# A decoder trunk in float32: the head casts older tiles before it modulates the newest, the bias rows are made at the start, and the fold's sums are copied one product later

## The chip, the cores and the metric

The kernel runs on one core of one Trainium2 chip. The metric is the device time of one execution in microseconds (us). Every time here comes from executions on the chip or from the profile of one of them.

## The reference

One layer of a decoder trunk on 2048 rows (tokens) of 1024 numbers, in float32, cut to what matters:

```python
mod = silu(c) @ w_ada + b_ada                 # one row of 3 * 1024
shift, scale, gate = split(mod, 3)
u = x * (1 + scale) + shift                   # (2048, 1024)
q, k, v, a_gate, p_in, p_gate, m_a, m_p = split(u @ w_in)
a = sliding_window_sink_attention(q, k, v, sinks, bias(rel_bias)) * silu(a_gate)
a = a @ w_attn_proj
p = grouped(multiscale_causal_pool(p_in), w_pool_mix)     # 4 groups of 256 x 256
p = (p * pool_scale * silu(p_gate)) @ w_pool_proj
y = ((sigmoid(m_a) * a + sigmoid(m_p) * p) @ w_out) * (1 + gate)
x = layer_norm(ALPHA * x + y)
```

The bias of attention depends on the distance of two tokens alone: 32 buckets of distances, one number for each bucket and head. `w_pool_mix` is small, and the kernel multiplies it into the pooling part of `w_in` once ("the fold"), so that no product is needed for it later.

## The kernel before

**Products.** A float32 operand is split into a high part (an ACT cast to the type fp32r) and a low part (a DVE subtraction). `mm3` adds three TensorE matmuls, hi x hi, hi x lo and lo x hi. The big products go through a scheme with seven products instead of eight for a 2 x 2 block matrix, so that sums of the blocks are needed on both sides. The moving sides are called B11, T1, T2, B21, T3, B22 and T4 ("sets"), each of four k tiles of 128 x 512, high and low. The still sides are the weights, two blocks of 128 columns at a time (a `Quad`), with three pairs of sums `first`, `second` and `third`, each split by one ACT cast and one DVE subtraction of 128 x 1024 into buffers named `w_set`; `mid` and `late` make the sums in between. A "product" below is one call of `product`: twelve matmuls of 128 x 512. The sequence is fixed (`front`, `back`, `ring`): a group is two quads, whose `front` makes four products (B11 and T1 for each), and whose `back` makes ten: T2 and B21 for each quad, T3 and B22 for each, then T4 for each.

**Order of the work.** After each product `tick()` runs the hooks that are written down for that place, among them all side work: the sums of the second half of x (`sums_to`, stored as k_hi and k_lo), the fold (`fold_parts`), the gate's modulation and the transposes of v (`turn`). `steps` places a list of (offset, function) from a start position, counted in ticks. The engines marked as ordered (`act`, `dve`, `pool`, `sp`, `pe`) keep the program's order; other instructions are placed by a scheduler when the program is built. Each engine then runs its own list in order and waits at semaphores. DMAs are issued from the queues of SP, POOL and ACT.

**The head** (`head`) makes the modulation and the sets for the first half of x. It goes through the eight k tiles. For tile k, TensorE makes the shift (sixteen small matmuls, `pe_modulation`) and DVE the scale (a reduction of 128 x 1024, in the trace CUSTOM_DVE_ANT_0, then a one-column addition). ACT then modulates the two halves of x (ACTIVATE, 128 x 512 twice). `closing(k - 2)` splits T of the tile two back, and `middle(k - 1)` makes the difference t of the halves of the tile before and splits its B. So in step k the order on ACT is: modulate k, cast T of k - 2, cast B of k - 1. Between them stand the first splits of the two opening quads (`pair_split`, after tile 1), their `mid`, the first four products and, at the end, `rest_sums`, the sums from which T3, T4 and B22 are split by hooks in the first group (ticks 1, 2 and 4). A copy of half of each of four tiles goes to memory by POOL's queue (b12_d, in the trace b_d).

**The bias rows** (`bias_rows`) are 32 small GpSimd operations on 16 partitions, one for each bucket, which fill a row of 384 numbers for each head (`et`), and a store of it to e_d; a hook at tick 3 of the first group runs them. Later hooks (`spread_bias`) spread e_d over the partitions.

**The fold** runs four times in the first phase (starts 14, 42, 70, 94). `fetch` loads the mix matrix (mr) and a half of the weights (wpt into a buffer named spare), `split` splits them, `fold` makes 48 short matmuls into the PSUM banks pv and pt, copies the sums out as st_hi (ACT) and st_lo (DVE) and stores these to wmix_d from POOL's queue. Buffers named c (five of them) serve st_hi, st_lo, mr, k_hi, k_lo, the gates and, in this version, the bias rows; two buffers named spare serve `sums_to`, the fold and the gate's modulation in turn.

Of the kernel before, what the change touches and what calls it, by code (L numbers as in the profile page):

```python
# [11 lines left out]
F32 = mybir.dt.float32  # L12
# [46 lines left out]
def kernel(  # L59
# [30 lines left out]
    def set_tile(pl, n):  # L90
        return pl.tile([P, 4, 2, CH], F32R, tag=f"set_{n}", name=f"set_{n}")

    sets = {n: set_tile(cp, n) for n in ("B11", "T1", "T2", "B21")}
    ident = cp.tile([P, P], F32, name="ident")
    mod = cp.tile([P, 24], F32, name="mod")
    nsink = cp.tile([P, HEADS], F32, name="nsink")
# [27 lines left out]
    def as32(ap):  # L124
        return ap.bitcast(F32)

    def low(engine, dst, src, hi):
        engine.tensor_tensor(dst, src, as32(hi), ALU.subtract)  # L128
# [85 lines left out]
    def sums_to(ph, store, i, load, work, b12):  # L214

        b = []

        def x(r, c):
            return b[r][:, c * CH : (c + 1) * CH]

        def fetch():
            b.extend((ph.spare(), ph.spare()))
            for r in range(2):
                load(b[r], r)

        def sub(out, a, c):
            return lambda: pool.tensor_tensor(x(*out), x(*a), x(*c), ALU.subtract)

        todo = [(0, fetch), (3, lambda: work(b[0], 0)), (3.5, lambda: work(b[1], 1))]
        todo += [(at, sub(*z)) for at, z in (  # L230
            (7.5, ((0, 1), (0, 1), (0, 0))),
            (9, ((1, 1), (1, 1), (0, 1))),
            (10.5, ((1, 0), (1, 0), (1, 1))),
            (12, ((0, 0), (1, 1), (0, 0))),
        )]
        for at, name, z in (
            (4, "B11", (0, 0)), (4.7, "B12", (0, 1)), (5.4, "B21", (1, 0)), (6.1, "B22", (1, 1)),
            (8.5, "T1", (0, 1)), (10, "T2", (1, 1)), (11.5, "T4", (1, 0)), (13, "T3", (0, 0)),
        ):
            if b12 or name != "B12":  # L240
                split, keep = kept_parts(ph, store[name][i], lambda z=z: x(*z))
                todo += [(at, split), (at + 1, keep)]
        return sorted(todo, key=lambda t: t[0])
# [377 lines left out]
                nc.scalar.copy(dst[:, 0, :], src)  # L621
                low(nc.vector, dst[:, 1, :], src, kk[kv * HD : kv * HD + HD, kv, 0, c0 : c0 + CH])

    def bias_rows(ph):
        rel = ph.t.tile([HEADS, BUCKETS], F32, tag="c", bufs=ph.bufs["c"], name="rel")
        nc.sync.dma_start(rel, relT)
        et = ph.t.tile([HEADS, ET], F32, tag="c", bufs=ph.bufs["c"], name="et")
        pool.memset(et, BIG)
        bk = buckets()
        for b in range(BUCKETS):  # L630
            ds = np.nonzero(bk == b)[0]
            if len(ds) == 0:
# [345 lines left out]
    def fold_parts(ph, g):  # L978

        m, r, w = [], [], []  # L980

        def fetch(half):
            if half == 0:
                r.append(ph.c("mr"))
                sp.dma_start(r[0], mix[g])
            r.append(ph.spare())
            sp.dma_start(r[-1], wpt[g, half])

        def split(half):
# [6 lines left out]
            act.copy(w[0], r[-1])  # L996
            low(dve, w[1], r[-1], w[0])

        def fold(half):
            mhi, mlo = m  # L1000
            hi, lo = w
            for i in range(0, 4, 2):
                acc = bank("pt" if i else "pv").rearrange("p (e c) -> p e c", e=2)
                for e in range(2):
                    for ct in range(2):
                        a0 = ct * CH + (i + e) * P
                        cols = slice(ct * 256, (ct + 1) * 256)
                        mm3(acc[:, e], hi[:, a0 : a0 + P], lo[:, a0 : a0 + P], mhi[:, cols], mlo[:, cols], ct == 0, ct == 1)
                src = acc.rearrange("p e (m d) -> p e m d", m=2)
                st = [ph.c(n, F32R).rearrange("p (m e d) -> p m e d", m=2, e=2) for n in ("st_hi", "st_lo")]  # L1010
                by = [x.rearrange("p m e d -> p e m d") for x in st]
                nc.scalar.copy(by[0], src)
                low(nc.vector, by[1], src, by[0])
                k = 4 * half + i
                for hl in range(2):
                    dst = wmix_d[2 * g : 2 * g + 2, :, hl, k : k + 2, :].rearrange("m p k d -> p m k d")
                    nc.gpsimd.dma_start(dst, as32(st[hl]))

        return (
            (0, lambda: fetch(0)),  # L1020
            (1, lambda: split(0)),
            (2, lambda: (fold(0), fetch(1))),
            (3, lambda: split(1)),
            (4, lambda: fold(1)),
        )

    def modulate(u, k):
# [28 lines left out]
    def head(ph):  # L1056
# [13 lines left out]
        act.dma_start(mod, bada)  # L1070
        act.dma_start(psc, pscale)
        act.dma_start(nsink, sinks.partition_broadcast(P))
        act.activation(sg, ct, AF.Sigmoid)
        dve.tensor_tensor(ct, ct, sg, ALU.mult)
        act.activation(late[0], cb, AF.Sigmoid)
# [24 lines left out]
        def modulation(k):  # L1100
            m = KT + k
            w = ws[k][1]
            dve.tensor_tensor_reduce(w, w, cb, 1.0, mod[:, m : m + 1], ALU.mult, ALU.add, mod[:, m : m + 1])
            dve.tensor_tensor(mod[:, k : k + 1], mod[:, k : k + 1], sums[k][:, 0:1], ALU.add)
            for x in xs[k]:
                act.activation(x, x, AF.Identity, bias=mod[:, k : k + 1], scale=mod[:, m : m + 1])

        def minus(dst, a, b):
            dve.tensor_tensor(dst, a, b, ALU.subtract)
# [35 lines left out]
        for k in range(KT):  # L1145
            load(k)
            if k < 2:
                grp[k].load(ph, False, sp, None)
        opening(0)
        opening(1)  # L1150
        middle(0)
        for q in grp:
            q.sum1(dve)
            starts.append(pair_split(ph, q.first(), act, dve))
        for k in range(2, KT):
            opening(k)
            closing(k - 2)
            middle(k - 1)
            if k in (2, 4):
                grp[k // 2 - 1].mid(pool, dve)  # L1160
            if 3 <= k < 7:
                products(k - 3)
            if k == 7:
                rest_sums(0)
        closing(6)
        middle(7)
        opened[0][3] = pair_split(ph, grp[0].second(), act, dve)
        closing(7)
        opened[1][3] = pair_split(ph, grp[1].second(), act, dve)
        for i in (3, 1, 2):  # L1170
            rest_sums(i)
        for q in grp:
            q.late(dve)
# [14 lines left out]
    def first_phase(ph, groups, turn, opened, cb, rest):  # L1188
        hooks = {}

        def at(group, pos, f):
            hooks.setdefault((group, pos), []).append(f)

        for g in range(4):
            steps(hooks, groups, (14, 42, 70, 94)[g], fold_parts(ph, g))
        for i in range(2):
            at(1, 1 + 2 * i, lambda i=i: turn(i))
        for j in range(KT):
            at(3 + j // 2, 3 + 5 * (j % 2), lambda j=j: spread_bias(j))
        for i in range(4):  # L1200
            ks = (i, 4 + i)
            todo = sums_to(
                ph,
                u1_d,
                i,
                lambda x, r, ks=ks: sp.dma_start(x, xt[1, ks[r]]),
                lambda x, r, ks=ks: modulate(x, ks[r]),
                True,
            )
            steps(hooks, groups, (1, 29, 57, 80)[i], todo)  # L1210
        for i in range(8):
# [160 lines left out]
```

## Time and profile before

| what | value |
|---|---|
| median of 3 runs | 1870.0 us (1867.99 to 1878.24) |
| the profiled execution | 1861.84 us |
| its span | 1860.1 us |
| PE (TensorE) busy | 1735.2 us, 93% |
| PEld (weight loads, beside PE) | 1436.4 us, 77% |
| DVE (VectorE) busy | 1315.5 us, 71% |
| ACT (ScalarE) busy | 938.5 us, 50% |
| POOL (GpSimd) busy | 935.5 us, 50% |
| DMA | 381.32 MB, mean 205 GB/s |

A line of the timeline reads: start and duration in us, engine, line of the program, operation, output <- input, shapes, count, and in brackets the engine's idle time before it and what ended it. The helper that records the ordered engines' operations is line 55, so most lines say L55, and the names of the tiles tell what it is. An entry such as "SPq" is the issue of a DMA on that queue. PE's busy time also covers time in which matmuls are queued but starved of weights.

### The profile page before, as it was taken

What the parts mean: (1) busy time and instruction counts of PE and PEld (TensorE: products, weight loads), DVE (VectorE), ACT (ScalarE), POOL (GpSimd) and SP (SyncE); (2) the same over time, 40 slices, a digit from 0 to 9 for tenths busy, and PEclk for the clock granted to TensorE, in tenths of its full rate; (3) what the DMA queues carried; (4) which work ended last, traced back from release to release, by engine and by line L of the source; (5) the groups of instructions that cost most, each with busy time, mean ns of one, the idle gap of its engine ahead of it and who ended that gap; (6) DMA issues with size and microseconds to landing.
All of it is one profiled execution on the core that took longest, in us unless ns stands there. A gap on an engine that the chain in (4) does not pass through costs nothing. (4 is left out here: it accounts for less than half of the span.)

```text
span 1860.1 us, 25320 instructions
## 1 busy us (share of the span) xinstructions
PE 1735.2 (93%) x8248; PEld 1436.4 (77%) x8248; DVE 1315.5 (71%) x2284; ACT 938.5 (50%) x1977; POOL 935.5 (50%) x758
## 2 busy tenths in 40 slices
PE   6689899989999999999999999999989989999996
PEld 6467777777888888787777788888867778777775
DVE  5776766544677787777666457777857887886886
ACT  3543434333777776544444457777724333422453
POOL 0454445433254677545445314556763785476543
PEclk9889999999999999999999999999999999999998
DMA  9245566766344447785777733544786574689432
GB/s 346 74 163 189 198 218 213 254 211 180 107 144 163 159 154 294 262 285 196 254 258 251 259 126 120 181 145 139 278 300 204 185 258 155 214 291 382 146 140 104
DMA packets 163571, 381.32 MB, mean 205 GB/s; under 512 B 19680, under 2 KB 23792, under 8 KB 163440
## 3 DMA queue, kind: packets, MB, share of 16 engines
q1 hardware_dynamic: 150560, 342.95, 52.9%
q0 software_dynamic: 10112, 33.06, 5.2%
q10 hardware_dynamic: 2768, 3.70, 0.9%
q8 instruction: 65, 1.06, 0.2%
q14 instruction: 66, 0.54, 0.1%
HBM read 244.35 MB, written 138.44 MB: 206 GB/s over the span
## 5 line engine op out<-in xcount | busy, mean ns | idle before, releaser
L55 PE MATMUL mm<-set_B,w_set 128*128 128x512 f32 x3240 | 804.1, 396 | 31.7 <-DVE w_set L128 24.3
L55 PEld LDWEIGHTS mm<-set_B,w_set 128*128 128x128 f32 x3240 | 602.2, 189 | 165.8 <-DVE w_set L128 33.5
L55 PE MATMUL lg<-set_T,w_set 128*128 128x512 f32 x2088 | 529.1, 403 | 61.9 <-ACT w_set L311 24.6
L55 PEld LDWEIGHTS lg<-set_T,w_set 128*128 128x128 f32 x2088 | 398.6, 193 | 168.9 <-ACT w_set L311 33.2
L128 DVE TENSOR_TENSOR w_set<-W,w_set 128x1024 fp32r<-128x1024 f32 x162 | 241.4, 1490 | 142.4 <-ACT w_set L311 137.2
L311 ACT CAST w_set<-W 128x1024 fp32r<-128x1024 f32 x162 | 169.3, 1049 | 239.0 <-PE mm L55 146.8
L55 PE MATMUL mm<-set_T,w_set 128*128 128x512 f32 x1080 | 269.0, 397 | 0.6 <-ACT set_T L55 0.3
L55 PEld LDWEIGHTS mm<-set_T,w_set 128*128 128x128 f32 x1080 | 202.3, 190 | 44.6 <-ACT set_T L55 1.5
L289 POOL TENSOR_TENSOR W<-W 128x512 f32<-128x512 f32 x56 | 81.3, 1451 | 158.5 <-DVE w_set L128 149.4
L283 POOL TENSOR_TENSOR W<-W 128x512 f32<-128x512 f32 x56 | 86.8, 1550 | 130.8 <-DVE w_set L128 114.4
L362 POOL TENSOR_TENSOR p<-p,u 128x512 f32<-128x512 f32 x58 | 98.8, 1705 | 104.5 <-DVE u L361 102.2
L55 DVE TENSOR_TENSOR o<-pv,o 64x128 f32<-64x128 f32 x256 | 72.4, 283 | 92.7 <-ACT o L55 89.9
L55 ACT ACTIVATE L<-L,nm 128x257 f32<-128x257 f32 (+1 forms) x256 | 127.2, 498 | 8.6 <-DVE nm L55 3.5
L55 DVE TENSOR_TENSOR k_lo<-spare,k_hi 128x512 fp32r<-128x512 f32 x88 | 90.0, 1029 | 47.0 <-ACT k_hi L55 14.8
L279 POOL TENSOR_TENSOR W<-W,A 128x512 f32<-128x512 f32 x56 | 83.8, 1496 | 74.9 <-DMA W<-in_win_dram 17.0
L55 DVE CUSTOM_DVE_ANT_0 L<-lg,bt,nsink 128x256 f32<-128x256 f32 (+1 forms) x256 | 111.6, 473 | 5.3 <-PE lg L55 1.3
L284 POOL TENSOR_TENSOR W<-W 128x512 f32<-128x512 f32 x56 | 90.0, 1607 | 13.4 <-DMA W<-in_win_dram 10.5
L55 POOL TENSOR_TENSOR w_set<-W,w_set 128x1024 fp32r<-128x1024 f32 x14 | 33.6, 2403 | 122.5 <-ACT w_set L55 89.6
L55 POOL TENSOR_TENSOR p<-nxt,pg 128x512 f32<-128x512 f32 x32 | 41.3, 1291 | 104.0 <-DVE sm L55 103.9
L55 ACT COPY o<-pv 64x256 f32<-64x256 f32 x128 | 47.2, 369 | 82.4 <-PE pv L55 80.3
L55 DVE TENSOR_TENSOR ptl<-pt,pth 128x512 fp32r<-128x512 f32 (+1 forms) x128 | 85.7, 670 | 1.7 <-ACT pth L55 1.6
L55 PE MATMUL lg<-kk,qs 128*128 128x256 f32 (+1 forms) x512 | 80.5, 279 | 0.0
(201 smaller groups left out, 2495.9 us busy)
## 6 DMA issues: line engine op xcount, KB each, us to landing
W<-in_win_dram SPq DMA_DIRECT2D x68, 256.0 KB, 3.7
w_set<-wmix_d SPq DMA_DIRECT2D x32, 512.0 KB, 5.3
A<-in_win_dram SPq DMA_DIRECT2D x34, 256.0 KB, 4.1
W<-in_win_dram POOLq DMA_DIRECT2D x34, 256.0 KB, 3.7
ag_d<-sig SPq DMA_DIRECT2D x32, 256.0 KB, 2.8
pg_d<-sig SPq DMA_DIRECT2D x32, 256.0 KB, 3.7
ma_d<-sig SPq DMA_DIRECT2D x32, 256.0 KB, 3.8
mp_d<-sig SPq DMA_DIRECT2D x32, 256.0 KB, 3.2
```

What stands on the lines that cost most here:

```text
L55: return lambda *args, **kw: self.tc.keep_in_program_order(op(*args, **kw))
L128: engine.tensor_tensor(dst, src, as32(hi), ALU.subtract)
L279: e.tensor_tensor(self.w[:, 1, :], self.w[:, 2, :], self.a22, ALU.add)
L283: e.tensor_tensor(x[:, 1, :], x[:, 1, :], x[:, 0, :], ALU.subtract)
L284: e.tensor_tensor(x[:, 2, :], x[:, 0, :], x[:, 2, :], ALU.subtract)
L289: e.tensor_tensor(x[:, 0, :], x[:, 0, :], x[:, 1, :], ALU.subtract)
L311: a.copy(by_two(hi), raw)
L362: nc.gpsimd.tensor_tensor(p5, p5, u2, ALU.add)
```

## The change

Three things are done.

1. In `head`, `modulation` no longer modulates x; a new function `modulate_x(k)` does, and it is called after `closing(k - 2)` and `middle(k - 1)`. The first splits of the two opening quads come after the casts of step 2 and no longer after tile 1; `mid` comes in steps 3 and 5, not 2 and 4. `rest_sums(0)` and `rest_sums(1)` come in steps 6 and 7, the other two after the loop. The hooks for T3, B22 and T4 move one tick forward, to ticks 0, 1 and 3.
2. `bias_rows` runs at the start of the head, right after the first small loads. It works in a tile that shares its place with the set T2, which is claimed only afterwards (`late_sets(cp, "T2")`), and loads its table through ACT's queue.
3. In `fold_parts`, `fetch(1)` comes one product after `fetch(0)`, ahead of the first split, and the copies and stores of the sums are a function `keep` of their own, called one product behind the matmuls. The starts become 13, 41, 69 and 92, so that the matmuls stand where they stood, but for the fourth fold, whose matmuls come one product earlier. In `sums_to`, the buffers are taken in the other order and row 1 is loaded first.

```diff
-    sets = {n: set_tile(cp, n) for n in ("B11", "T1", "T2", "B21")}
+    sets = {n: set_tile(cp, n) for n in ("B11", "T1", "B21")}
@@ sums_to
             b.extend((ph.spare(), ph.spare()))
-            for r in range(2):
+            b.reverse()
+            for r in (1, 0):
                 load(b[r], r)
@@
-    def bias_rows(ph):
-        rel = ph.t.tile([HEADS, BUCKETS], F32, tag="c", bufs=ph.bufs["c"], name="rel")
-        nc.sync.dma_start(rel, relT)
-        et = ph.t.tile([HEADS, ET], F32, tag="c", bufs=ph.bufs["c"], name="et")
+    def bias_rows():
+        room = cp.tile([P, 4 * D], F32, tag="set_T2", name="head_T2")
+        rel, et = room[0:HEADS, 0:BUCKETS], room[0:HEADS, D : D + ET]
+        act.dma_start(rel, relT)
         pool.memset(et, BIG)
@@ fold_parts
+        accs = []
         def fold(half):
...
+                accs.append((4 * half + i, acc))
...
+        def keep():
+            for k, acc in accs:
                 src = acc.rearrange("p e (m d) -> p e m d", m=2)
...
-                nc.scalar.copy(by[0], src)
-                low(nc.vector, by[1], src, by[0])
+                act.copy(by[0], src)
+                low(dve, by[1], src, by[0])
...
-                    nc.gpsimd.dma_start(dst, as32(st[hl]))
+                    pool.dma_start(dst, as32(st[hl]))
+            accs.clear()
-            (1, lambda: split(0)),
-            (2, lambda: (fold(0), fetch(1))),
-            (3, lambda: split(1)),
-            (4, lambda: fold(1)),
+            (1, lambda: fetch(1)),
+            (2, lambda: split(0)),
+            (3, lambda: fold(0)),
+            (4, lambda: (keep(), split(1))),
+            (5, lambda: fold(1)),
+            (6, keep),
@@ head
+        bias_rows()
+        late_sets(cp, "T2")
         act.activation(sg, ct, AF.Sigmoid)
...
+        def modulate_x(k):
             for x in xs[k]:
-                act.activation(x, x, AF.Identity, bias=mod[:, k : k + 1], scale=mod[:, m : m + 1])
+                act.activation(x, x, AF.Identity, bias=mod[:, k : k + 1], scale=mod[:, KT + k : KT + k + 1])
...
         opening(0)
+        modulate_x(0)
         opening(1)
         middle(0)
-        for q in grp:
-            q.sum1(dve)
-            starts.append(pair_split(ph, q.first(), act, dve))
+        modulate_x(1)
         for k in range(2, KT):
             opening(k)
             closing(k - 2)
             middle(k - 1)
-            if k in (2, 4):
+            if k == 2:
+                for q in grp:
+                    q.sum1(dve)
+                    starts.append(pair_split(ph, q.first(), act, dve))
+            modulate_x(k)
+            if k in (3, 5):
                 grp[k // 2 - 1].mid(pool, dve)
             if 3 <= k < 7:
                 products(k - 3)
-            if k == 7:
-                rest_sums(0)
+            if k > 5:
+                rest_sums(k - 6)
...
-        for i in (3, 1, 2):
+        for i in (3, 2):
             rest_sums(i)
@@ first_phase
-            steps(hooks, groups, (14, 42, 70, 94)[g], fold_parts(ph, g))
+            steps(hooks, groups, (13, 41, 69, 92)[g], fold_parts(ph, g))
...
-        for n, f in zip((1, 2, 4), rest):
+        for n, f in zip((0, 1, 3), rest):
             at(0, n, f)
-        at(0, 3, lambda: bias_rows(ph))
```

More of the change, by code (lines that the diff above doesn't have):

```diff
@@ L995, in split @@
             w[:] = ph.split(), ph.split()
-            act.copy(w[0], r[-1])
-            low(dve, w[1], r[-1], w[0])
+            act.copy(w[0], r[1 + half])
+            low(dve, w[1], r[1 + half], w[0])
+        accs = []
         def fold(half):
@@ L1011, in fold @@
                 by = [x.rearrange("p m e d -> p e m d") for x in st]
-                nc.scalar.copy(by[0], src)
-                low(nc.vector, by[1], src, by[0])
-                k = 4 * half + i
+                act.copy(by[0], src)
+                low(dve, by[1], src, by[0])
                 for hl in range(2):
                     dst = wmix_d[2 * g : 2 * g + 2, :, hl, k : k + 2, :].rearrange("m p k d -> p m k d")
-                    nc.gpsimd.dma_start(dst, as32(st[hl]))
+                    pool.dma_start(dst, as32(st[hl]))
+            accs.clear()
         return (
             (0, lambda: fetch(0)),
-            (1, lambda: split(0)),
-            (2, lambda: (fold(0), fetch(1))),
-            (3, lambda: split(1)),
-            (4, lambda: fold(1)),
+            (1, lambda: fetch(1)),
[4 more added lines that the diff above has]
+            (6, keep),
         )
```

## The prediction

> **What bounds the kernel now.** I read the page first, then the busy time by stretches, then the timeline of the first 140 us engine by engine, then what ended TensorE's idle time in the first phase.
>
> ```profile
> span 1860.1 us, 25320 instructions
> 40.00:50.00 10.00, 9.48 (x55) 7.91 (x54) 6.17 (x11) 4.78 (x8) 0.55 (x1) 0.94 0.50 196
> 50.00:60.00 10.00, 2.74 (x21) 2.49 (x19) 5.82 (x13) 5.09 (x8) 0.00 (x0) 0.74 0.00 0
> 60.00:70.00 10.00, 6.40 (x17) 4.64 (x18) 10.00 (x16) 6.33 (x11) 0.00 (x0) 0.58 0.00 1
> 80.00:90.00 10.00, 5.00 (x18) 3.56 (x18) 8.94 (x13) 1.82 (x3) 10.00 (x29) 0.95 0.26 89
> ```
>
> The columns are stretch, length, busy PE, PEld, DVE, ACT, POOL, granted clock, DMA share, GB/s. Most of the span belongs to TensorE, but here it is idle: 7.3 us of 50 to 60, 3.6 of 60 to 70, 5.0 of 80 to 90. The DMA share from 50 on is 0, so loads do not bound the first hole. Neither DVE nor ACT is full there; they wait for each other. In 80 to 90 POOL is full, for the only time in the table. All edits lie in this stage or at the four folds, so the sum is made there; everything behind it stands in the same order.
>
> One step k of the head, and where the steps end:
>
> ```profile
> 50.02 1.28 DVE L55 CUSTOM_DVE_ANT_0 head_kk<-head_kk,cb,mod 128x1024 f32<-128x1024 f32 x1
> 51.41 1.52 ACT L55 ACTIVATE head_vv<-head_vv,mod 128x512 f32<-128x512 f32 x2 [2.71 <-DVE mod L55]
> 52.84 0.60 ACT L55 CAST set_T<-t 128x512 fp32r<-128x512 f32 x1
> 53.47 0.69 DVE L55 TENSOR_TENSOR set_T<-t,set_T 128x512 fp32r<-128x512 f32 x1 [2.09 <-ACT set_T L55]
> 54.08 0.68 DVE L55 TENSOR_TENSOR t<-A,t 128x512 f32<-128x512 f32 x1
> 54.68 0.69 DVE L55 TENSOR_TENSOR set_B<-head_kk,set_B 128x512 fp32r<-128x512 f32 x1
> 55.28 1.28 DVE L55 CUSTOM_DVE_ANT_0 head_kk<-head_kk,cb,mod 128x1024 f32<-128x1024 f32 x1
> 61.75 0.69 DVE L55 TENSOR_TENSOR set_T<-t,set_T 128x512 fp32r<-128x512 f32 x1
> 64.83 4.23 PE L55 MATMUL lg<-set_T,w_set 128*128 128x512 f32 x10 [1.41 <-DVE w_set L55]
> ```
>
> A step is 55.28 - 50.02 = 5.26 us. DVE reduces (1.39 to the start of the modulation), stands 2.09 us while ACT first modulates tile k and only then casts the older T tile, and subtracts three half tiles, 0.60 us apart (53.47 to 55.28 is 1.81). The ten matmuls at 64.83 are the first work TensorE gets behind the head, and DVE's subtraction of w_set releases them.
>
> **The head's order of casts.** In the changed program ACT casts T of k-2 and B of k-1 before it modulates k. Both inputs are there since the step before, so the casts run under DVE's reduction, the modulation runs under DVE's three subtractions, and the 2.09 goes. What is late next is DVE itself: 1.39 + 1.81 = 3.20 us a step. ACT's own step, 1.52 + 0.60 + 0.60, is 2.7, so it keeps up. Two quad splits also move behind step 2, and the `mid` subtractions to steps 3 and 5. For these:
>
> ```profile
> 20.65 3.58 PE L55 MATMUL lg<-ct,head_T 128*128 128x1 f32 x16 [2.86 <-DMA head_T<-in_wadat_dram]
> 20.69 0.68 DVE L55 TENSOR_TENSOR W<-W,A 128x512 f32<-128x512 f32 x1
> 26.56 1.28 DVE L55 CUSTOM_DVE_ANT_0 head_T<-head_T,cb,mod 128x1024 f32<-128x1024 f32 x1
> 31.82 1.28 DVE L55 TENSOR_TENSOR W<-W 128x512 f32<-128x512 f32 x2
> 33.03 1.28 DVE L55 CUSTOM_DVE_ANT_0 head_T<-head_T,cb,mod 128x1024 f32<-128x1024 f32 x1
> 34.48 0.33 SPq L55 DMA_DIRECT2D head_vv<-in_xt_dram  x1
> head_vv<-in_xt_dram SPq DMA_DIRECT2D x2, 512.0 KB, 10.7
> ```
>
> The two splits hold DVE from 20.69 to 26.56, 5.87 us, now while it waits for tile 2's weights. Moved, they lose that cover. Step 2 cannot finish before TensorE's sums for it do, 20.65 + 3.58 = 24.2, 24.4 with the addition; three subtractions make 26.2, the splits 32.1. So step 3 starts at 32.1 against 33.03, only 0.9 sooner. From there: five steps at 3.20 are 16.0; two `mid` pairs at 1.21 (31.82 to 33.03) are 2.4; `rest_sums` 0 and 1, four half tiles, are 2.4. DVE reaches the last-but-one T subtraction at 32.1 + 20.8 = 52.9. The same count for before, 33.03 + 5 x 5.26 + 1.21 + 1.20, gives 61.7, the row's 61.75. Gain so far 8.8 us. Loads: tile 7's x lands at 34.48 + 10.7 = 45.2, and its step begins at about 48.5, so they stay hidden, by 3 us. TensorE then starts at 64.83 - 8.8 = 56.0.
>
> **The bias rows and the rest of the splits.**
>
> ```profile
> 72.76 3.41 POOL L362 TENSOR_TENSOR p<-p,u 128x512 f32<-128x512 f32 x1 [27.07 <-DVE u L361]
> 76.13 1.21 DVE L128 TENSOR_TENSOR w_set<-W,w_set 128x1024 fp32r<-128x1024 f32 x1
> 77.05 2.92 PE L55 MATMUL lg<-set_T,w_set 128*128 128x512 f32 x12
> 78.95 11.27 POOL L55 TENSOR_SCALAR et<-rel 16x1 f32<-16x1 f32 x32
> 82.27 1.30 DVE L55 TENSOR_TENSOR set_B<-A,set_B 128x512 fp32r<-128x512 f32 x2
> 83.02 2.82 PE L55 MATMUL mm<-set_B,w_set 128*128 128x512 f32 x11 [2.82 <-DVE set_B L55]
> 88.49 4.15 PE L55 MATMUL lg<-set_T,w_set 128*128 128x512 f32 x10 [2.18 <-DVE w_set L128]
> 90.25 0.62 ACT L55 CAST k_hi<-spare 128x512 fp32r<-128x512 f32 x1 [2.29 <-POOL et L55]
> 100.75 0.63 PE L55 MATMUL mm<-set_B,w_set 128*128 128x512 f32 x2
> 209.89 1.30 POOL L55 TENSOR_TENSOR spare<-spare 128x512 f32<-128x512 f32 x1
> ```
>
> The bias rows, 32 operations in 11.27 us on POOL, go to the start of the head. The issue of two b12 stores and the `mid` loads stand behind them there; those loads are issued at about 36 and later, so POOL has room. The rows are made in the place that the set T2 takes later, whose first write comes after 40 us; their store is long done by then. Their small table load goes to ACT's queue ahead of the first sigmoid, in the shadow of the first weights.
>
> At the first group of products the splits of T3 and B22 move one product earlier. B22's wait of 2.82 goes, but the built order now has all of T3, B22 and T4 ahead of the third pair's w_set on DVE, and a gate product that needs the second quad's B21. From 56.0 DVE does 25 half tiles at 0.60 (15.0) and two w_sets at 1.2: the pair is ready at 73.4. TensorE's four products, 77.05 - 64.83 = 12.2, end at 68.2. A new wait of 5.2 us takes the place of 2.82 and 2.18. After it ten matmuls cost 4.15, as after 88.49, and five products follow at 2.70 (92.64 to 100.75 is three): 73.4 + 17.7 = 91.1 against 100.75. Gain 9.7.
>
> A rule that speaks against the move: the Trainium skill, SBUF — State Buffer, section "Who interferes with whom", says that a VectorE instruction with two SBUF inputs and a GpSimd instruction that reads SBUF block each other for a whole instruction. The trace has it for large tiles, POOL taking 3.41 at 72.76 where the same shape takes 1.30 at 209.89. For the small rows it does not: DVE's two-input pair at 82.27 took 1.30 in the midst of them, 0.65 each. If the rule held DVE for a row of 0.35 (11.27 / 32) at each of some eight operations in the head's first 20 us, the sum would be up to 2.8 us worse; by the row it is 0, which I take.
>
> **Folds and the first group behind.**
>
> ```profile
> 115.16 3.75 PE L55 MATMUL lg<-set_T,w_set 128*128 128x512 f32 x10 [1.82 <-DVE w_set L128]
> 127.34 1.22 PE L55 MATMUL lg<-set_T,w_set 128*128 128x512 f32 x2 [4.82 <-ACT w_set L311]
> 136.95 0.69 DVE L128 TENSOR_TENSOR st_lo<-pt,st_hi 128x512 fp32r<-128x512 f32 x1 [0.75 <-ACT st_hi L1012]
> 138.88 0.60 PE L55 MATMUL pt<-ident,vt 128*128 128x128 f32 x4
> 212.79 0.39 SPq L55 DMA_DIRECT2D spare<-in_wpt_dram  x1
> 221.14 0.73 PE L55 MATMUL lg<-set_T,w_set 128*128 128x512 f32 x2 [2.92 <-ACT w_set L311]
> 312.99 0.73 PE L55 MATMUL lg<-set_T,w_set 128*128 128x512 f32 x2 [1.58 <-ACT w_set L311]
> 394.30 0.73 PE L55 MATMUL lg<-set_T,w_set 128*128 128x512 f32 x2 [3.42 <-ACT w_set L311]
> ```
>
> At each fold TensorE waits for a w_set cast that stands on ACT behind the fold's own split. The first such wait is 4.82, where the others are 2.92, 1.58 and 3.42: the chain of k_hi that the bias rows held up (2.29 at 90.25) ends late there. Without them I take the 2.92 for it, a gain of 1.9 (ends 0 and 4.82), and half of the 1.82 at 115.16, 0.9. The fold's loads move one store pair earlier in SP's queue. The spare that they need is free at 209.89 + 1.30 = 211.2, where the load goes out at 212.79: up to 1.6 sooner, at three folds up to 4.8 in all, at least 0. I take half, 2.4. The copies of the sums: in the built order the same neighbours stand before and after them on ACT, so they cost and bring nothing.
>
> **The sum.** 9.7 + 2.8 + 2.4 = 14.9 us. The profiled execution took 1861.84 (span 1860.1), which becomes 1847; it is 8 under the median of 1870.0, so against that I forecast 1855.
>
> **The rivals.** First, the gain is spent in DVE's queue. The pair that I put at 73.4 sits behind operations that POOL can stretch, as its own 3.41 shows for the other side. If T3 starts no sooner than now, at 77.05, the group still loses its two later waits: 77.05 + 17.7 = 94.7, a gain of 6, and with the chains behind as late as now the time is 1864. For it: DVE was full from 60 to 70. Against it: POOL has two operations there. 0.17; the case that the new order leaves no trace at all is counted here.
>
> Second, slower: the copies held back. If they do run a product later, the next writer of the two PSUM banks waits. Now the last copy ends at 136.95 + 0.69 = 137.64 and the transposes into that bank run at 138.88, a room of 1.2 us. A product is 2.70; if each of eight folds costs a whole one, 21.6 eat the 12.5 of the other parts: 1879. It decides from 1.6 us a fold. Against it: the unchanged neighbours on ACT. 0.08.
>
> **How the numbers follow.** My forecast has 0.75. Its top gain is 9.7 + 1.8 + 4.8 + 4.8, 21 us, or 1849. The three runs lie between 1868 and 1878, so a median of as many can lie some 4 to 6 us off: the range is 1843 to 1868, from that top gain less 6 to the first rival plus 4. Only the second rival is left out. The bound of what a measurement can tell is 0.5%, 9.4 us: faster 0.74, same 0.18, slower 0.08.
>
> **What would show it.** Right: no 2.09 wait for set_T from step 3 on, steps of 3.2 us, TensorE's ten matmuls near 56, one wait of about 5 us near 68 to 74 for w_set, none near 83, front products at about 91. Wrong: steps still over 4 us, the pair later than 77, or waits in front of the transposes at the folds.

## The result, and the profile after

The changed kernel takes 1850.26 us (median of 4 runs, 1849.77 to 1854.1), before in the same comparison 1868.99 (median of 4, 1861.73 to 1878.24): a ratio of 0.9917, 95% interval 0.9895 to 0.9939, or 0.8% faster. The forecast was 1855, with a gain of 14.9 us; the medians differ by 18.7, and the ratio, by which all runs are compared here, makes 15.5 of 1869 (11.4 to 19.6 by its interval). The profiled execution took 1849.77 us.

First the busy time by stretches of the kernel after (the columns are those of the prediction's fence):

```profile
span 1848.0 us, 25300 instructions
...
50.00:60.00 10.00, 6.09 (x14) 4.31 (x15) 10.00 (x16) 8.06 (x14) 0.00 (x0) 0.51 0.00 1
60.00:70.00 10.00, 8.75 (x38) 6.89 (x36) 8.74 (x16) 6.63 (x12) 5.00 (x2) 0.98 0.45 159
80.00:90.00 10.00, 10.00 (x45) 8.18 (x44) 9.60 (x10) 5.11 (x10) 4.85 (x4) 1.00 0.32 117
```

From 50 to 60 DVE is now full, where it was busy 5.82 of 10, and TensorE is busy 6.09 and no longer 2.74. From 80 to 90 TensorE has no hole at all, and POOL is half free.

The timeline of the kernel after, from the head to the end of the first group's ten products. (They are made by `back`; the prediction calls them front products. The row at 91.86 is the first product behind them.)

```profile
9.04 7.97 POOL L55 TENSOR_SCALAR head_T<-head_T 16x1 f32<-16x1 f32 x32 [7.37 <-DMA head_T<-in_relT_dram]
...
42.99 1.29 DVE L55 CUSTOM_DVE_ANT_0 head_kk<-head_kk,cb,mod 128x1024 f32<-128x1024 f32 x1
...
44.48 0.69 DVE L55 TENSOR_TENSOR set_T<-t,set_T 128x512 fp32r<-128x512 f32 x1
...
47.50 1.28 DVE L55 CUSTOM_DVE_ANT_0 head_kk<-head_kk,cb,mod 128x1024 f32<-128x1024 f32 x1
...
55.13 4.63 PE L55 MATMUL lg<-set_T,w_set 128*128 128x512 f32 x10 [1.20 <-DVE w_set L55]
...
74.20 4.06 PE L55 MATMUL lg<-set_T,w_set 128*128 128x512 f32 x10 [5.45 <-DVE w_set L128]
...
91.86 2.94 PE L55 MATMUL mm<-set_B,w_set 128*128 128x512 f32 x12
```

The subtraction for set_T at 44.48 has no wait in brackets; before, it stood 2.09 us there. This step has two half tiles of `rest_sums` in it, so 47.50 - 42.99 = 4.51 is 3.31 without them (0.60 each). TensorE starts its ten matmuls at 55.13 (forecast 56.0, before 64.83). One wait of 5.45 follows (forecast 5.2), and the ten products end at 91.86 (forecast 91.1, before 100.75). This part came out as it was reckoned.

Then the waits at the folds in the kernel after:

```profile
117.70 1.22 PE L55 MATMUL lg<-set_T,w_set 128*128 128x512 f32 x2 [5.08 <-ACT w_set L312]
...
151.72 0.73 PE L55 MATMUL mm<-set_B,w_set 128*128 128x512 f32 x2 [1.70 <-ACT w_set L312]
153.24 4.63 PE L55 MATMUL mm<-set_B,w_set 128*128 128x512 f32 x10 [0.80 <-DVE w_set L128]
...
215.27 0.73 PE L55 MATMUL lg<-set_T,w_set 128*128 128x512 f32 x2 [3.09 <-ACT w_set L312]
...
251.16 4.14 PE L55 MATMUL mm<-set_B,w_set 128*128 128x512 f32 x10 [0.85 <-DVE w_set L128]
...
398.02 0.39 PE L55 MATMUL pv<-mhi,w_set 128*128 128x256 f32 x1 [0.54 <-ACT w_set L55]
```

The 4.82 in front of the first fold did not become 2.92; it is 5.08. Behind the second half of the first fold stands a wait that was not forecast, 1.70 and 0.80, and the ten matmuls behind it take 4.63 us. In the kernel before, the row at that place shows one wait of 1.15, and 2.57 us for the ten matmuls:

```profile
162.13 2.57 PE L55 MATMUL mm<-set_B,w_set 128*128 128x512 f32 x10 [1.15 <-DVE w_set L128]
```

The same pair of waits stands behind the second and third fold. The 3.42 in front of the fourth fold is gone. So the total came out near the forecast, but its terms behind 92 us did not, and the experiments ask about those.

### The profile page after: what moved, and what is told of

The parts are those of the page before. It is cut to its first block, busy times and chain, and to the rows that moved or that the text cites. A ratio compares the mean times of both kernels' runs of the same rounds, so it can differ in the third digit from the quotient of the medians.

```text
span 1848.0 us, 25300 instructions
## 1 busy us (share of the span) xinstructions
PE 1732.7 (94%) x8248; PEld 1437.6 (78%) x8248; DVE 1312.4 (71%) x2284; ACT 942.6 (51%) x1977; POOL 928.6 (50%) x758
## 5 line engine op out<-in xcount | busy, mean ns | idle before, releaser
L55 PE MATMUL lg<-set_T,w_set 128*128 128x512 f32 x2088 | 523.0, 400 | 49.5 <-ACT w_set L312 18.2
L285 POOL TENSOR_TENSOR W<-W 128x512 f32<-128x512 f32 x56 | 90.0, 1610 | 12.1 <-DMA W<-in_win_dram 9.5
L55 ACT CAST k_hi<-spare 128x512 fp32r<-128x512 f32 x88 | 53.6, 616 | 55.2 <-POOL spare L55 20.3
```

The lines of the kernel that those rows point to most:

```text
L55: return lambda *args, **kw: self.tc.keep_in_program_order(op(*args, **kw))
L285: e.tensor_tensor(x[:, 2, :], x[:, 0, :], x[:, 2, :], ALU.subtract)
```

## The experiments

Each kernel ran beside the kernel before, in the same comparison. Its ratio is to that.

| run | what is in it | median us | before | ratio, 95% interval |
|---|---|---|---|---|
| e1 | new head, early bias rows | 1851.95 | 1867.53 | 0.9921 (0.9899 to 0.9944) |
| e2 | fold part alone | 1869.44 | 1867.53 | 1.0004 (0.9985 to 1.0022) |
| e3 | bias rows alone | 1869.04 | 1867.53 | 1.0014 (0.9996 to 1.0032) |
| e4 | new head alone | 1854.15 | 1867.53 | 0.9932 (0.9906 to 0.9958) |
| e5 | the whole change again | 1854.31 | 1869.43 | 0.9912 (0.9892 to 0.9932) |
| e6 | change, copies with their fold | 1849.14 | 1869.43 | 0.9897 (0.9878 to 0.9917) |
| e7 | change, stores from ACT's queue | 1854.34 | 1869.43 | 0.9917 (0.9901 to 0.9932) |
| e8 | e1, folds split a product later | 1839.90 | 1869.43 | 0.9841 (0.9824 to 0.9858) |
| e9 | change, stores placed freely | 1844.55 | 1865.55 | 0.9892 (0.9876 to 0.9909) |
| e10 | change, T3, B22, T4 a tick later | 1851.67 | 1865.55 | 0.9927 (0.9912 to 0.9942) |
| e11 | e8, fourth fold a product sooner | 1834.65 | 1865.55 | 0.9823 (0.9799 to 0.9848) |
| e12 | e11 with the ticks of e10 | 1833.90 | 1865.55 | 0.9827 (0.9807 to 0.9847) |

**The three parts, one at a time (e1 to e4).** The theory that these began with: the head brings the gain, and the fold's late copies hold the buffers named c and give some of it back.

```diff
# e1: of the change, without
-            b.reverse()
-            for r in (1, 0):
+            for r in range(2):
... fold_parts as before
-            steps(hooks, groups, (13, 41, 69, 92)[g], fold_parts(ph, g))
+            steps(hooks, groups, (14, 42, 70, 94)[g], fold_parts(ph, g))
# e2: before, with these same parts as changed
# e3: before, with bias_rows() at the start of the head and its place in T2
# e4: e1, with bias_rows(ph) at tick 3 of the first group as before
```

> The changed kernel with the fold, the order of sums_to and the fold's starts as before; only the new head and the early bias rows are left of the change. In the changed kernel the lead over before is 10.5 us at the first fold's short matmuls and 6.0 at the second fold's. Theory A (the copies held back keep the buffers named c, so the lead is lost behind each fold): here the lead stays between 9 and 11 at the second and third fold, the wait in front of the mm product behind the second half of each fold is 1.0 to 1.3 us and not 1.70 + 0.80, and the fourth fold's wait of 3.4 is back; the time is 1847 to 1853, within 4 us of the changed kernel on either side. Theory B (the lead itself is what is lost, because the loads behind it are no earlier): the lead falls to about 6 at the second fold here too, and the time is 1853 to 1858.

> The kernel before with only the fold's part of the change (copies one product later, both loads early, starts 13, 41, 69 and 92, sums_to in the other order). Theory A: 1 to 2 us are lost behind each of the first three folds and about 5 come back at the fourth: within 3 us of before in all, with new waits behind the second half of the first three folds. Theory B: nothing is lost behind the folds and the gain at the fourth stands alone: 4 to 6 us faster than before. The prediction's reckoning was 2.4 faster.

> The kernel before with only the bias rows made at the start of the head. By the prediction the chain of k_hi starts 2.3 us earlier, the 1.82 before the product at 115 halves and the 4.82 at the first fold becomes 2.92: 2.8 us faster. Rival: the chain at the first fold is held by the buffers named c and not by POOL, so that the 4.82 stays as in the changed kernel (5.08): 0 to 1 us faster. If the 32 small operations hold up the head's first steps, the first products come later than 64.83: slower by up to 2.8.

> The kernel before with only the new order in the head (older tiles cast first, splits after step 2, mid in steps 3 and 5, T3, B22 and T4 split a product earlier); the bias rows stay on GpSimd at tick 3 of the first group. By the prediction the ten T2 matmuls start near 56 and the first group's front of products ends about 9 us sooner: 8 to 10 us faster than before. Rival (the bias rows, now in the midst of the moved sums, hold them up): the pair for the third sums comes 2 us or more later than 74 and the time is 5 to 7 us under before.

The head alone makes 0.9932, 12.7 us of 1867.53 (interval 7.8 to 17.6); the 8 to 10 expected lie inside, below the middle. The head with the bias rows makes 0.9921, the whole change 0.9912 and 0.9917: the fold part adds nothing that can be told, and alone it makes 1.0004. The 4 to 6 us of e2's theory B are excluded by its interval (its lower end is 2.8 us). The bias rows alone bring nothing (1.0014; its lower end allows 0.7 us). What became of their 2.8 is seen in the timeline of e3, ACT's chain and then TensorE at the first fold:

```profile
119.11 0.62 ACT L55 CAST k_hi<-spare 128x512 fp32r<-128x512 f32 x1 [2.16 <-DMA u_T_split<-k_hi]
121.16 0.62 ACT L55 CAST mhi<-mr 128x512 fp32r<-128x512 f32 x1 [1.43 <-DMA mr<-in_mix_dram]
...
123.95 1.04 ACT L311 CAST w_set<-W 128x1024 fp32r<-128x1024 f32 x1
...
125.04 1.22 PE L55 MATMUL lg<-set_T,w_set 128*128 128x512 f32 x2 [5.65 <-ACT w_set L311]
```

k_hi waits for a store to give a buffer back, the fold's split waits for the load of the mix matrix, and the cast of w_set that TensorE needs stands behind both. GpSimd is not in this chain. The wait is 5.65, not 2.92.

In e1 the wait behind the second half of the first fold is back to one of 1.45:

```profile
149.73 2.57 PE L55 MATMUL mm<-set_B,w_set 128*128 128x512 f32 x10 [1.45 <-DVE w_set L128]
```

So the new waits belong to the fold part. e2 has them too, 1.54 + 0.79, 2.17 + 0.86 and 2.79 + 0.53 behind the first three folds, and 0.84 where 3.42 stood in front of the fourth. Loss and gain come to nothing in sum, which fits theory A of e2 in the waits and the time; what makes the waits is asked next.

In the change the wait in front of the first fold has a longer chain than in e3. The last cast of k_hi ahead of the fold's split, on ACT:

```profile
114.61 0.62 ACT L55 CAST k_hi<-spare 128x512 fp32r<-128x512 f32 x1 [6.74 <-DMA u_T_split<-k_hi]
```

The store that it waits for was issued at 108.94, behind the first two loads of the fold. When this cast is done, the mix matrix and the weights are there, and no further wait stands before the cast of w_set at 116.60. In e4 the waits of the same chain are 1.63 for the store, then 1.76 and 1.38 for the two loads. Nothing here separates the bias rows from the rest in time: e1 and e4 differ by 2.2 us, with intervals that overlap.

**What in the fold part costs (e5 to e7, e9).** e5 repeats the change so that it stands in the same comparison.

```diff
# e6: the change, with
-            (3, lambda: fold(0)),
-            (4, lambda: (keep(), split(1))),
-            (5, lambda: fold(1)),
-            (6, keep),
+            (3, lambda: (fold(0), keep())),
+            (4, lambda: split(1)),
+            (5, lambda: (fold(1), keep())),
# e7: the change, with
-                    pool.dma_start(dst, as32(st[hl]))
+                    act.dma_start(dst, as32(st[hl]))
```

> The changed kernel once more, on the same chip and beside the same runs of before as the three that follow, to have it in one comparison with them. 0.990 to 0.994 of before; the lead over before's profile at the second fold's short matmuls (226.31 there) is about 6, and ten matmuls behind the wait of 1.70 + 0.80 take 4 us and more, not 2.6.

> The changed kernel with one thing undone: each copy and store of the fold's sums is made right behind its own fold, not one product later; the early second load and the starts stay. Theory A (the held copies put their stores behind GpSimd's next sum, which waits for a load, so the buffers named c come free too late): the waits of 1.70 + 0.80, 1.83 + 0.85 and 2.78 + 0.53 behind the second half of the first three folds go back to one of 1.0 to 1.3, the product after them to 2.6 us, and the lead over before at the second fold stays at 10 us or more; first attention matmul 3 to 6 us sooner than in the changed kernel. Theory B (the early load or the other starts do it): the waits stay, and the time is the changed kernel's within 1 us.

> The changed kernel with the stores of the fold's sums issued from ACT's queue and no longer from GpSimd's; the copies stay one product late. Theory A: the stores of the second half go out some 2 us behind their copies and not behind GpSimd's sum, 3 to 4 us sooner than now; the activation that waited 9.15 us for a buffer waits less than 6, and the waits 1.70 + 0.80 shrink to below 1.5 in sum. Rival (a copy one product late is itself too late, on whatever queue its store goes): the waits stay within 0.5 us of what they are. What the issues cost on ACT is small: four of 0.7 us for each half.

e5 has the new waits again (1.46 + 0.80 and 4.09 us for the ten matmuls). Its lead at the second fold is 226.31 - 217.21 = 9.1 and not 6. The expectation took a place in one profile for a property of the kernel: two executions of the same program stand 3 us apart there. From here on waits are compared, and stretches that begin and end at the same work.

e6 went against theory A at the first fold. With the copies called right behind their fold, waits of 1.49 + 0.80 still stand there; behind the second there are one of 1.52 and one of 1.21. The time, 0.9897, is 3 us below that of e5, with intervals that overlap. The timeline of GpSimd in e6 at the first fold shows why:

```profile
139.63 1.65 POOL L280 TENSOR_TENSOR W<-W,A 128x512 f32<-128x512 f32 x1 [10.97 <-DVE st_lo L55]
141.22 0.72 POOL L55 DMA_DIRECT2D wmix_d<-st_hi  x1
```

(The end of this wait is put down to a subtraction on DVE; at e6's second fold, where it is 10.82, to the load of A, as in the change.) Neither the copies nor the stores are sooner than in the change. The two copies of the first fold's second half start 1.64 and 3.95 us behind the half's first matmul in e6, 1.63 and 3.98 in the change, and 1.64 and 3.96 in the kernel before: called a product later, they came no later at the first three folds, as the prediction had it. The first store goes out 7.6 us behind the half's start in e6, 6.9 in the change, and 2.5 before. It stands behind GpSimd's sum for the next weights, because `pool` keeps the written order where before the scheduler placed the stores (`nc.gpsimd`). In e7, where the stores leave by ACT's queue, the wait behind the second half is gone (no wait from 132 to 197 us), and the activation that waited 9.15 us for a buffer waits 0.91. But now ACT's casts stand behind the issues, and TensorE waits between the halves instead:

```profile
129.46 0.74 PE L55 MATMUL lg<-set_T,w_set 128*128 128x512 f32 x2 [2.11 <-ACT w_set L312]
131.12 4.08 PE L55 MATMUL lg<-set_T,w_set 128*128 128x512 f32 x10 [0.92 <-DVE w_set L128]
```

Its time is that of the change. A third theory, C, came out of these two: neither the copies nor the loads make the waits behind the folds, but the place of the stores in GpSimd's queue. e9 tests it with one word.

```diff
# e9: the change, with
-                    pool.dma_start(dst, as32(st[hl]))
+                    nc.gpsimd.dma_start(dst, as32(st[hl]))
```

> The changed kernel with one word changed: the stores of the fold's sums are left to the scheduler again, as before, and no longer bound to the written order of GpSimd. The copies still come one product late. In the built order three of the four stores of a second half then stand ahead of GpSimd's sum for the next weights, not behind it. Theory C (it is the place of the stores in GpSimd's queue that costs, not the late copies): the activation that waited 9 us for a buffer named c waits less than 4, the waits 1.70 + 0.80, 1.83 + 0.85 and 2.78 + 0.53 shrink to one of 1.0 to 1.5 each, the product after them takes 2.6 us, and the first attention matmul comes 3 to 6 us before the changed kernel's 458.9 to 460.3. Rival (the copies are too late themselves): the waits stay, and the time is that of the changed kernel within 1 us.

The view of waits from 120 to 460 us (engine and tile that waits, what it waits for, us in total, times, longest), first of the change, then of e9:

```profile
POOL W L280 <- DMA A<-in_win_dram: 35.4, 4, 10.7
...
ACT sig L517 <- DMA wmix_d<-st_lo: 27.8, 3, 9.8
...
DVE c L387 <- DMA wmix_d<-st_hi: 17.1, 3, 6.3
...
POOL wmix_d L55 <- ACT st_hi L55: 4.2, 4, 3.3
```

```profile
POOL wmix_d L1023 <- ACT st_hi L55: 28.5, 10, 7.5
...
ACT sig L517 <- DMA wmix_d<-st_lo: 4.7, 3, 2.0
...
POOL W L280 <- DMA A<-in_win_dram: 4.5, 4, 1.4
...
DVE c L387 <- DMA wmix_d<-st_hi: 1.4, 2, 0.8
```

The chain is in these lines. GpSimd waits up to 10.7 us for a load; the stores stand behind it; ACT and DVE wait for the buffers that the stores read; the cast of w_set that TensorE needs stands behind them on ACT. With the stores ahead of the sum, the waits of ACT and DVE for these buffers fall from 44.9 us in sum to 6.1. GpSimd's own wait does not shrink, it changes place: 28.5 us ahead of the stores and 4.5 ahead of the sum, 33.0 in all, where the change has 4.2 and 35.4. The timelines at the first fold, of the change and then of e9:

```profile
138.82 1.29 POOL L280 TENSOR_TENSOR W<-W,A 128x512 f32<-128x512 f32 x1 [10.59 <-DMA A<-in_win_dram]
140.06 0.73 POOL L55 DMA_DIRECT2D wmix_d<-st_hi  x1
...
149.12 0.63 ACT L517 ACTIVATE sig<-c 128x512 f32<-128x512 f32 x1 [9.15 <-DMA wmix_d<-st_lo]
```

```profile
134.99 0.73 POOL L1023 DMA_DIRECT2D wmix_d<-st_hi  x1 [7.45 <-ACT st_hi L55]
...
139.42 1.29 POOL L280 TENSOR_TENSOR W<-W,A 128x512 f32<-128x512 f32 x1 [1.37 <-DMA A<-in_win_dram]
...
140.12 0.63 ACT L517 ACTIVATE sig<-c 128x512 f32<-128x512 f32 x1 [0.87 <-DMA wmix_d<-st_lo]
...
151.32 2.57 PE L55 MATMUL mm<-set_B,w_set 128*128 128x512 f32 x10 [1.57 <-DVE w_set L128]
```

The first store goes out 2.5 us behind the start of the fold's second half (132.47) and no longer 6.9 (133.18 to 140.06). TensorE's wait is one of 1.57 and the ten matmuls take 2.57; behind the second and third fold it is one of 0.77 and one of 1.23. The copies start 1.63 and 3.98 us behind the half's first matmul, as in the change. So theory C holds for the mechanism. In time e9 makes 0.9892 against 0.9912 and 0.9917, some 4 us with intervals that overlap: the direction is as expected, the size is not settled. In the profile its first attention matmul comes at 445.81, 13 us before e5's 458.9 and more than expected; it also ran the stretch from 300 to 400 at a granted clock of 1.00 where e5 had 0.98.

**The wait in front of the folds (e8, e11).** The chain of e3 says that w_set waits on ACT for the fold's own load. e8 leaves the loads where they are and takes the splits a product later, on the base of e1.

```diff
# e8: e1, with
-            (1, lambda: split(0)),
-            (2, lambda: (fold(0), fetch(1))),
-            (3, lambda: split(1)),
-            (4, lambda: fold(1)),
+            (2, lambda: (split(0), fetch(1))),
+            (3, lambda: fold(0)),
+            (4, lambda: split(1)),
+            (5, lambda: fold(1)),
...
-            at(1, 1 + 2 * i, lambda i=i: turn(i))
+            at(1, 2 + 2 * i, lambda i=i: turn(i))
# e11: e8, with the fourth fold's start at 93 and not at 94
```

> The new head and the early bias rows with the fold of before, but each fold's loads are issued where they were and its splits and short matmuls come one product later (and the two transposes of v one product later too). It asks what the wait in front of each fold is: w_set stands on ACT behind the fold's own split, which waits for a load that is issued 5 to 6 us before. If that is so, the waits of 3.52, 2.83, 1.51 and 3.50 us in front of the four folds fall below 1 each, the products behind them go from about 4 us to 2.6, and the first attention matmul comes 8 us or more before 454.8; 1842 to 1848 us. Rival (the next product's cast is late in any case): the waits move by one product and stay as long; 1850 to 1854.

> As the run with the splits a product later, but the fourth fold starts at 93 and not at 94, so that its short matmuls are where they were before and only its loads and the stores come sooner. There a wait of 3.08 stood behind that fold, and the twelve matmuls after it took 5.99. If the fold's stores, a product later than before, held the buffers named c there, the wait falls to 0.5 to 1 and the product to 3 us, and the first attention matmul comes at 434 to 437 instead of 440.75: 0.981 to 0.983 of before. Rival (the wait goes back to the front of the fold, 3.5 us as in the kernel before): no gain, 0.984 to 0.986.

The timeline of TensorE at the product in front of the first fold, e1 and then e8:

```profile
114.01 0.79 PE L55 MATMUL lg<-set_T,w_set 128*128 128x512 f32 x2 [3.52 <-ACT w_set L311]
```

```profile
109.46 0.61 PE L55 MATMUL lg<-set_T,w_set 128*128 128x512 f32 x2
110.36 2.57 PE L55 MATMUL lg<-set_T,w_set 128*128 128x512 f32 x10 [0.29 <-DVE w_set L128]
```

In e8 the waits of 3.52, 2.83 and 1.51 in front of the first three folds are gone, and 3.50 in front of the fourth is 0.74. The first attention matmul comes at 440.75, 14.0 us before e1's 454.79, and the time is 1839.9 us, a little under the 1842 to 1848 expected; its ratio, 0.9841, has an interval apart from that of the change. Not all went as expected: behind the first three folds waits of 1.96 to 2.66 stand where e1 has 1.1 to 1.5, and at the fourth one of 3.08 is new. e11 asked about that one. The timeline of TensorE behind the fourth fold, e8 and then e11:

```profile
388.29 5.99 PE L55 MATMUL mm<-set_B,w_set 128*128 128x512 f32 x12 [3.08 <-ACT w_set L311]
```

```profile
393.14 0.73 PE L55 MATMUL mm<-set_B,w_set 128*128 128x512 f32 x2 [0.60 <-ACT w_set L311]
394.50 2.57 PE L55 MATMUL mm<-set_B,w_set 128*128 128x512 f32 x10 [0.63 <-DVE w_set L128]
```

The wait is 0.60 and the twelve matmuls take 3.3 us (0.73 + 2.57) and not 5.99, as expected. The first attention matmul did not come at 434 to 437 but at 443.68: this execution was behind e8's by 3.2 us at the first fold already. The time, 0.9823, is in the expected span, but its interval overlaps e8's.

**The wait of 5.45 in the first group (e10, e12).**

```diff
# e10: the change, with
-        for n, f in zip((0, 1, 3), rest):
+        for n, f in zip((1, 2, 4), rest):
# e12: e11 with the same
```

> The changed kernel with the splits of T3, B22 and T4 in the first group back at ticks 1, 2 and 4. In the built order of DVE both subtractions of the third pairs then stand right behind T3 and ahead of B22 and T4. If the wait of 5.45 is DVE's queue, as the prediction counted it (25 half tiles and two subtractions from 56.0 to 73.4), it falls below 1 us, and what is late next is B22, behind a modulation of 128 x 1024 of a loaded tile: a wait of 2 to 4 us at the product after, the front products 1 to 3 us sooner than 91.9. Rival (the waits only change places, as the prediction had it for the kernel before: 2.82 and 2.18): the front products end within 1 us of 91.9.

> The two runs before this in one kernel: splits of the folds a product later, the fourth fold at 93, and T3, B22 and T4 split at ticks 1, 2 and 4. If the two effects are apart in time, as they lie (60 to 90 us and 110 to 400 us), their gains add: the time of the run with the fourth fold at 93 less what the later splits bring, 1 to 3 us: 0.980 to 0.982 of before, 1833 to 1837 us. Rival (what the first group gains is waited for again at the first fold): the same time as the run with the fourth fold at 93.

The timeline of TensorE in e10:

```profile
74.44 4.37 PE L55 MATMUL mm<-set_B,w_set 128*128 128x512 f32 x11 [2.77 <-DVE set_B L55]
...
115.08 1.22 PE L55 MATMUL lg<-set_T,w_set 128*128 128x512 f32 x2 [8.32 <-ACT w_set L312]
```

The 5.45 is gone and B22 is late next, by 2.77: the wait was DVE's queue, as the prediction counted it. The row that stands at 91.86 in the change starts at 89.72, 2.1 sooner. But the first fold waits 8.32 and not 5.08: most of the gain is waited for there, and 0.9927 is the time of the change. e12 repeats it where the folds are split later, and its 0.9827 is e11's 0.9823. That does not show the rival: the 1 to 3 us expected are less than these intervals can tell. The profiles leave it open too. In e12 the fold's first matmul waits 1.47 for DVE where e11 waits 0.28, and it comes 60.9 us behind the ten T2 matmuls (54.69 to 115.57), against 63.5 in e11 (55.66 to 119.17) and 61.2 in e8 (54.73 to 115.96).

The best versions are e11 and e12: 1834.65 and 1833.9 us, 0.982 and 0.983 of before, against 0.991 for the change.

## Why the prediction was right, and where not

- **The head (8.8 us): right.** The 2.09 went, the steps are DVE's alone, its last-but-one T subtraction stands at 52.05 (forecast 52.9), and TensorE's ten matmuls start 64.83 - 55.13 = 9.7 us sooner. (Two matmuls of the same product stand ahead of the ten, at 62.20 before and 52.71 after; the prediction calls the ten the first.)
- **The first group (9.7): right.** The wait of 5.45 stands where 5.2 was forecast, and the lead behind the ten products is 100.75 - 91.86 = 8.9. e10 shows its cause, DVE's order. In time the head alone is worth 12.7 (7.8 to 17.6), so 9.7 lies inside, below the middle.
- **The bias rows (2.8): wrong.** The step that failed is "Without them I take the 2.92 for it". It took the first chain seen to wait for GpSimd (2.29 at 90.25) for the one that sets the fold's wait. e3 removed GpSimd from it and the wait is 5.65; e4, with the bias rows left where they were, is nearest to 2.92, with 3.11. What sets it in e3 and e4 is the fold's split on ACT, behind a store and two loads: e8 moved the split back and the wait went. Of the other part, 0.9 for half of the 1.82 at 115.16, e3 shows 0.4: the wait there is 1.44. That the small rows hold up nothing was right: in the head they took 7.97 us, 0.25 each, and the start of T2 in e3, 64.75, is that of before, 64.83. The rule of the Trainium skill that was weighed against it (SBUF — State Buffer, section "Who interferes with whom") would have put that start up to 2.8 us later; no run here shows it.
- **The fold's loads (2.4): not found.** The fold part alone makes 1.0004. The loads do go out sooner: at the second fold 0.6 us behind the sum that frees their buffer (203.82 + 1.30 to 205.75) and not 1.6. But the waits in front of the second and third fold are 3.09 and 1.38, where they were 2.92 and 1.58. At the first fold the early loads stand ahead of a store of k_hi in SP's queue, which the prediction did not count among what the loads move past: with the new head the wait is 4.64 to 5.51 where both loads are early (the change, e5, e6, e7, e9; 8.32 in e10, which reaches the fold sooner), and 3.52 and 3.11 where they are not (e1, e4). That this store is the reason is read from the order of issues and the 6.74 us that a k_hi cast waits for it; no run changed it alone, and the new order in `sums_to` came and went with it.
- **The copies ("cost and bring nothing"): right for the copies, wrong for what hangs on them.** The reason given was "the same neighbours stand before and after them on ACT". That was so but for one activation, which in the change runs ahead of the second half's copies, and at the first three folds the copies came no later than before; but each copy ends in a store, and the store's neighbours on GpSimd were not compared. In the change it was bound to GpSimd's written order, behind a sum that waits 10.6 us for a load. e9 shows it.
- **The fourth fold: not in the sum.** Its matmuls come a product earlier, and the 3.42 before them became 0.54. The sum had nothing for it; with e2 at 1.0004 it about paid for the waits behind the three other folds.
- **The rivals.** The gain was not spent in DVE's queue: the pair came at 74.20. The slower rival priced the held copies at the PSUM banks, with a wait in front of the transposes; none is there, and the copies came no later. What did cost were their stores, through the buffers named c.

So the mechanism was right for the head and the first group, but that 14.9 came out as 15.5 is partly luck. By the two profiles the lead is 8.9 us behind the first group, 10.4 at the first attention matmul (470.70 and 460.29) and 12.1 at the end (1861.84 and 1849.77). The 5.2 us of the other terms came out near nothing, and no row accounts for the gain beyond these leads; the interval of the ratio, 11.4 to 19.6 us, is wider than those terms.

## What to carry to other kernels

When a copy is moved, follow it to the end: its store, the queue that issues the store, what stands ahead of it there, and who waits for the buffer that the store reads. A store left to a scheduler and one bound to an engine's written order are two different places, and one word decides. And where an engine waits in front of a side task's first product, look at what that task puts ahead of the main work's cast: moving the split back by one product, behind its load, was worth about as much here as the whole change (0.9841 in e8 against 0.9921 in e1, some 15 us).

## What the runs showed of the hardware

In these runs a wait of TensorE could cost more than its length, because the granted clock fell behind it. The busy time by stretches, from the start of the first fold's second half to the second fold, so the same work in each: of before, of the change and of e9 (the column ahead of the DMA share is the granted clock):

```profile
143.69:226.31 82.62, 76.86 (x338) 62.04 (x336) 58.71 (x63) 32.99 (x50) 38.58 (x31) 0.98 0.59 202
```

```profile
133.18:220.27 87.09, 80.00 (x337) 63.98 (x336) 55.65 (x63) 33.26 (x50) 38.43 (x31) 0.94 0.55 191
```

```profile
132.47:213.95 81.48, 77.14 (x338) 62.19 (x337) 58.91 (x63) 33.11 (x50) 39.40 (x31) 0.98 0.59 205
```

The change takes 4.5 us longer than before; 1.3 of it is idle time (87.09 - 80.00 against 82.62 - 76.86), the other 3.1 is the same matmuls at 0.94 and not 0.98 (80.00 x 0.94 and 76.86 x 0.98 are both 75.2 to 75.3). Right behind the new wait the clock is lower still, in the change, and in e8 after a wait of 2.66 it is not:

```profile
150.00:158.00 8.00, 5.50 (x14) 4.09 (x14) 7.80 (x11) 4.49 (x7) 2.24 (x2) 0.66 0.44 164
```

```profile
142.00:149.00 7.00, 6.51 (x29) 5.37 (x30) 6.18 (x9) 3.09 (x5) 3.41 (x3) 1.00 0.50 164
```

The Trainium skill, TensorE: Matmul & The Clock Gate, section "Part 1: The HAM clock gate", says that the clock halves after an idle window of some 3.4 us and that this window runs free, so that the same kernel meets it differently from run to run. The trace agrees on the half: from 153 to 158 us the granted clock of the change is 0.50. The runs agree that the length of the wait alone doesn't decide (4.63 us for ten matmuls behind 1.70 + 0.80 and 4.09 behind 1.97 in e11, but 2.58 behind 2.66 in e8). They differ in that less than 3.4 us of idle time was enough, and here the measurement decides.
